# A hybrid decoder trunk on one core: the mLSTM matmuls of the sample tokens widened from 64 or 32 rows to 128

## The chip, the cores and the metric

The kernel runs on one core of one Trainium2 chip. The metric is the device time of one execution in microseconds (us). The core has five engines with instruction queues of their own: TensorE (PE in the profile; its weight loads are listed as PEld), VectorE (DVE), ScalarE (ACT), GpSimd (POOL) and SyncE (SP), which issues all the DMAs here.

## The reference

One decoder layer is computed for two groups of tokens with shared weights: a prompt of 256 tokens, and 8 samples with 8 new tokens each. So there are 320 tokens, of model width 2048, all in fp32.

```python
x1 = layer_norm(ALPHA * x + 0.5 * swiglu_ffn(x, ffn1_w1, ffn1_w3, ffn1_w2), ln1_g, ln1_b)
q, k, v, o, ig, fg, glu_a, glu_b, gate_a, gate_b = jnp.split(x1 @ w_in, SPLIT_IDX, axis=-1)
h_a, (C_new, n_new, m_new) = mlstm_branch(q, k, v, o, ig, fg, b_igate, b_fgate, mh_norm_g, C0, n0, m0, chunk)
h_b, conv_new = conv_branch(glu_a, glu_b, conv_buf, conv_w, conv_b, conv_ln_g, conv_ln_b)
mix = (sigmoid(gate_a) * h_a + sigmoid(gate_b) * h_b) @ w_out
x2 = layer_norm(ALPHA * x1 + mix, ln2_g, ln2_b)
y = layer_norm(ALPHA * x2 + 0.5 * swiglu_ffn(x2, ffn2_w1, ffn2_w3, ffn2_w2), ln3_g, ln3_b)
```

The part that the change touches is the mLSTM branch. For each of 4 heads (keys of 256, values of 512) and each chunk of tokens:

```python
s = einsum('bhtd,bhsd->bhts', q, k) * d            # d: masked decay, per sequence
num = einsum('bhts,bhsv->bhtv', s, v) + w_inter[..., None] * einsum('bhtd,bhdv->bhtv', q, C0)
qn = sum(s, axis=-1) + w_inter * einsum('bhtd,bhd->bht', q, n0)
h = num / maximum(abs(qn), exp(-m_t))[..., None]
C_new = w_c[..., None, None] * C0 + einsum('bhs,bhsd,bhsv->bhdv', w_k, k, v)
```

The prompt starts with an empty state. Each sample has a state `C0` of 256 x 512 numbers per head that is read, used, updated and written: 8 samples x 4 heads = 32 states of 512 KB in and 32 out.

## The kernel before

**Layout.** Activations are held transposed, 128 features x 320 tokens per tile. The weights stream from HBM in chunks of 8 blocks of 128 x 128 (`Stream`, lines 114 to 166; 512 KB each). Each chunk is split on the chip into a high part (`whi`, ACT, line 146) and a remainder (`wlo`, DVE, line 147), both of the type fp32r. A product of one weight block is three matmuls (`mm3`, lines 211 to 213): high x high, high x low, low x high. These three lines, called the weight matmuls below, write PSUM tiles `acc` of 128 x 320.

**Order.** `ffn`, `mixer`, `out_proj`, `ffn` follow each other. Inside `mixer` the weight matmuls of `w_in` run, and after each 4 blocks (12 matmuls) `tick` (line 188) takes one step of each of four lanes: lane 0 holds `gates` and then the four `head`s, lane 1 the norms, lanes 2 and 3 the convolutions of even and odd feature tiles, which run on DVE (line 611, one tap per step). A step ends at a `yield`. Where a later group needs a result, `drain` steps the lanes until it is there; the output gates `o` of a head wait so for that head (line 934). On top of this written order a scheduler of the framework rearranges instructions within each engine when the program is built. Its result is fixed: each engine runs its instructions in that order.

**One head** (`head`, line 647). `rb` holds four rows of factors broadcast over partitions. `sp` (line 677) are the products of keys and queries: two blocks of 128 prompt keys, and one block for the 64 sample tokens; `dt` is the masked decay, `pt` their product, and `ph`, `pl` its two parts. `tv` (line 712) are the transposed values, split into `vt`. `qn` (lines 731 to 749) is the normaliser. `cp` (line 762) makes the prompt's new state. `vst` and `kst` (lines 778 and 787) are values and weighted keys of the samples, each sample's 8 tokens and their remainder parts in a group of 32 partitions: 4 samples per `vst` tile, two tiles. Then for each of the 8 samples: `ip` (line 810, 4 matmuls) is the query times the old state, whose split parts are `chi` (ACT) and `clo` (DVE); `cps` (line 815, 2 matmuls) is the update of the state; DVE adds it to the old state (line 816); SP writes the state (line 820) and loads the one after next (line 657). State tiles `c0` come from a pool tag with three buffers, which the input tiles `xraw` (line 333) and some others also use. Last, `num` (line 833 through `mm3`, and line 836) adds the two parts of the numerator, for 4 blocks of 128 value columns.

The sample tokens have 64 rows where they are the contracted axis of a matmul (`num`, `qn`, and the last of the cumulative sums `bp`), and `cps` has 32:

```python
mm(cp, kst[r, g, j * P:(j + 1) * P], vst[g][r, :], start=True, stop=True, tile_position=(32 * i, 0))
```

The profile writes such a shape as rows*columns of the stationary operand: `32*128` here, `64*128` for `num` and `qn` of the samples, `128*32` for `ip`, `128*128` for the weight matmuls.

Of the kernel before, what the change touches and what calls it, by code (L numbers as in the profile page):

```python
# [35 lines left out]
SEGW = HIST + NS  # L36

# [131 lines left out]
class Kernel:  # L169
# [181 lines left out]
    def consts(self, cp):  # L351
        nc, a = self.nc, self.a
        cst = cp.tile([P, C_N], F32, name="cst")
        nc.sync.dma_start(out=cst, in_=a["cst"])
        self.ident = cst[:, C_ID:C_ID + P]
        self.tri = cst[:, C_TRI:C_TRI + P]
        self.btri = cst[:TS, C_BTRI:C_BTRI + TS]
# [48 lines left out]
        nc.vector.tensor_copy(self.sel, cst[:ROWS, C_SEL:C_SEL + H * P])  # L406
# [95 lines left out]
    def gates(self, g8):  # L502
# [144 lines left out]
    def head(self, h, q, k, v):  # L647
# [61 lines left out]
        for i, n in enumerate((P, P, TS)):  # L709
# [4 lines left out]
            nc.scalar.activation(x[0][:n], tv[:n], AF.Copy)  # L714
# [18 lines left out]
        for x in (ph, pl):  # L733
            mm(qn[:, SEQ:], one[:TS, :], x[:TS, 384:], start=x is ph, stop=False)
# [433 lines left out]
```

## Time and profile before

| | |
|---|---|
| times shown | 2999.9, 3186.01 and 2992.91 us, median 2999.9 us |
| profiled execution | 2996.54 us, its span 2994.8 us |
| mean granted TensorE clock | 0.988 |
| PE busy | 2940.2 us, 98% of the span, 19580 matmuls |
| DVE busy | 1893.9 us, 63% |
| ACT busy | 1340.8 us, 45% |
| DMA | 460.32 MB, mean 154 GB/s |

A row of a timeline gives the start from the beginning of the span and the duration, both in us. Matmuls overlap: the end of one lies behind the start of the next, and its end is modelled. What a matmul costs the stream is therefore the distance from its start to the start of the next. Rows of a table of stretches give, for each engine, the busy time in the stretch and the instructions that started or ran in it; `PEclk` is the granted clock of TensorE, 1.00 at full speed. Groups of instructions are `line engine operation out<-in, shape, xcount | busy us, mean ns of one | idle before`.

### The profile page before, as it was taken

What the parts mean: (1) busy time and instruction counts of PE and PEld (TensorE: products, weight loads), DVE (VectorE), ACT (ScalarE), POOL (GpSimd) and SP (SyncE); (2) the same over time, 40 slices, a digit from 0 to 9 for tenths busy, and PEclk for the clock granted to TensorE, in tenths of its full rate; (3) what the DMA queues carried; (4) which work ended last, traced back from release to release, by engine and by line L of the source; (5) the groups of instructions that cost most, each with busy time, mean ns of one, the idle gap of its engine ahead of it and who ended that gap; (6) DMA issues with size and microseconds to landing.
All of it is one profiled execution on the core that took longest, in us unless ns stands there. A gap on an engine that the chain in (4) does not pass through costs nothing.

```text
span 2994.8 us, 50339 instructions
## 1 busy us (share of the span) xinstructions
PE 2940.2 (98%) x19580; PEld 2883.3 (96%) x19580; DVE 1893.9 (63%) x3498; ACT 1340.8 (45%) x2392; POOL 70.7 (2%) x76
## 2 busy tenths in 40 slices
PE   9999999999999999999999989999999999999997
PEld 9999999999998998989999889999999999999997
DVE  5544444444459999979989876578544444444447
ACT  5434433433445545545544545445433433433444
POOL 0100000000000000000000000200100000000001
PEclk9999999999999999999999989999999999999999
DMA  6444444444444456464555634444444444444443
GB/s 220 152 150 148 150 153 148 149 150 152 148 149 140 127 162 211 151 201 124 175 184 154 210 109 141 148 148 134 151 152 148 148 152 151 148 150 152 149 148 106
DMA packets 163136, 460.32 MB, mean 154 GB/s; under 512 B 50128, under 2 KB 52944, under 8 KB 162896
## 3 DMA queue, kind: packets, MB, share of 16 engines
q1 hardware_dynamic: 162896, 457.10, 47.2%
q8 instruction: 153, 2.51, 0.4%
q14 instruction: 87, 0.71, 0.1%
HBM read 433.29 MB, written 23.74 MB: 153 GB/s over the span
## 4 chain that ended last, share of the span: by engine, by line
PE 96%; DVE 2%; DMA 1%; ACT 1%; issue 0%; DVEq 0%; SPq 0%; ACTq 0%
PE acc L211 31%; PE acc L212 31%; PE acc L213 31%; PE ip L810 1%; PE cps L815 1%; DMA out_C_s<-c 0%; PE num L836 0%; PE num L211 0%; DVE wlo L147 0%; DMA c<-in_C 0%; PE num L213 0%; PE num L212 0%; DVE z L1083 0%; DVE z L473 0%; DVE xl L488 0%; ACT th L246 0%
## 5 line engine op out<-in xcount | busy, mean ns | idle before, releaser
L147 DVE TENSOR_TENSOR wlo<-wraw,whi 128x512 fp32r<-128x512 f32 x1568 | 1080.9, 691 | 924.4 <-ACT whi L146 918.8
L146 ACT ACTIVATE whi<-wraw 128x512 fp32r<-128x512 f32 x1568 | 987.7, 631 | 1453.4 <-PE acc L212 1342.8
L211 PE MATMUL acc<-xh,whi 128*128 128x320 f32 x4480 | 1392.7, 311 | 20.5 <-ACT th L246 9.6
L212 PE MATMUL acc<-xl,whi 128*128 128x320 f32 x4480 | 1390.7, 311 | 6.6 <-DVE xl L488 6.6
L213 PE MATMUL acc<-xh,wlo 128*128 128x320 f32 x4480 | 1387.6, 311 | 1.8 <-DVE wlo L147 1.8
L211 PEld LDWEIGHTS acc<-xh,whi 128*128 128x128 f32 x4480 | 847.4, 189 | 30.0 <-ACT th L246 10.5
L212 PEld LDWEIGHTS acc<-xl,whi 128*128 128x128 f32 x4480 | 847.2, 189 | 15.4 <-DVE xl L488 7.9
L213 PEld LDWEIGHTS acc<-xh,wlo 128*128 128x128 f32 x4480 | 844.8, 189 | 10.4 <-issue 3.9
L211 PE MATMUL acc<-hh,whi 128*128 128x320 f32 x1408 | 433.9, 309 | 0.3 <-ACT whi L146 0.3
L212 PE MATMUL acc<-hl,whi 128*128 128x320 f32 x1408 | 433.7, 309 | 0.0
L213 PE MATMUL acc<-hh,wlo 128*128 128x320 f32 x1408 | 432.5, 309 | 0.0
L211 PEld LDWEIGHTS acc<-hh,whi 128*128 128x128 f32 x1408 | 264.4, 188 | 0.6 <-ACT whi L146 0.6
L212 PEld LDWEIGHTS acc<-hl,whi 128*128 128x128 f32 x1408 | 264.2, 188 | 0.0
L213 PEld LDWEIGHTS acc<-hh,wlo 128*128 128x128 f32 x1408 | 263.9, 188 | 0.0
L611 DVE SCALAR_TENSOR_TENSOR cy<-pu,cw,cy 128x256 f32<-128x256 f32 x480 | 221.2, 476 | 1.0
L435 DVE SCALAR_TENSOR_TENSOR z<-acc,z 128x320 f32<-128x320 f32 x128 | 62.5, 488 | 54.5 <-PE acc L213 52.8
L211 PE MATMUL acc<-mh,whi 128*128 128x320 f32 x256 | 79.1, 309 | 0.0
L212 PE MATMUL acc<-ml,whi 128*128 128x320 f32 x256 | 79.0, 309 | 0.0
L213 PE MATMUL acc<-mh,wlo 128*128 128x320 f32 x256 | 78.7, 309 | 0.0
L313 POOL TENSOR_TENSOR z<-xh,xl 128x320 f32<-128x320 f32 x48 | 60.7, 1272 | 632.3 <-DVE h L425 351.7
L425 DVE TENSOR_TENSOR h<-s,acc 128x320 f32<-128x320 f32 x86 | 42.0, 488 | 52.2 <-ACT s L423 52.2
L423 ACT ACTIVATE s<-acc 128x320 f32<-128x320 f32 x86 | 37.7, 438 | 69.2 <-PE acc L213 69.2
(285 smaller groups left out, 1673.6 us busy)
## 6 DMA issues: line engine op xcount, KB each, us to landing
wraw<-in_wst SPq DMA_DIRECT2D x783, 512.0 KB, 3.3
c<-in_C SPq DMA_DIRECT2D x32, 512.0 KB, 4.1
out_C_s<-c SPq DMA_DIRECT2D x32, 512.0 KB, 4.8
out_yT<-z SPq DMA_DIRECT2D x16, 160.0 KB, 1.8
out_C_p<-cn SPq DMA_DIRECT2D x4, 512.0 KB, 2.9
us<-in_cache SPq DMA_DIRECT2D x16, 120.0 KB, 3.7
out_conv_s<-us SPq DMA_DIRECT2D x16, 120.0 KB, 6.0
xraw<-in_xT SPq DMA_DIRECT2D x3, 480.0 KB, 5.3
```

The source lines that it names most:

```text
L146: nc.scalar.activation(hi, raw, AF.Copy)
L147: nc.vector.tensor_tensor(out=lo, in0=raw, in1=hi.bitcast(F32), op=ALU.subtract)
L211: mm(ps, hi, xh, start=first, stop=False)
L212: mm(ps, hi, xl, start=False, stop=False)
L213: mm(ps, lo, xh, start=False, stop=last)
L313: self.nc.gpsimd.tensor_tensor(out=t, in0=hi.bitcast(F32), in1=lo.bitcast(F32), op=ALU.add)
L423: nc.scalar.activation(s, accs[2 * j], AF.Silu)
L425: nc.vector.tensor_tensor(out=hh, in0=s, in1=accs[2 * j + 1], op=ALU.mult)
L435: nc.vector.scalar_tensor_tensor(out=z[m], in0=ps, scalar=0.5 / ALPHA, in1=z[m], op0=ALU.mult, op1=ALU.add)
L611: nc.vector.scalar_tensor_tensor(out=yp, in0=pu[:, w:w + SEQ], scalar=self.cw[:, i, w:w + 1], in1=yp, op0=ALU.mult, op1=ALU.add)
L810: mm(ip[:32, :], qc[j][:, bs], x, start=j == 0 and n == 0, stop=j == 1 and n == 1)
L815: mm(cp, kst[r, g, j * P:(j + 1) * P], vst[g][r, :], start=True, stop=True, tile_position=(32 * i, 0))
```

## The change

The 64 sample tokens are no longer a third tile of 64 rows. The third tile is now the last 128 of the 320 tokens (`TILES = (0, P, T - P)`): 64 prompt tokens that also stand in the second tile, and the 64 sample tokens. The mask `btri` becomes a 128 x 128 tile that is zero outside the samples' corner, so that the prompt's rows in the third tile count for nothing. So `sp`, `dt`, `pt`, `ph`, `pl`, `tv`, `vt`, the samples' part of `qn` and `num`, and the gates' small products work on 128 partitions; several pairs of instructions (384 columns on 128 partitions, 64 columns on 64) become one of 448 columns. For `cps`, four constant tiles `kst` of 128 x 512 are zeroed once in `consts`; each head's `ks` is copied by four ACT instructions of 32 partitions into the band of the tile that belongs to the sample, and the matmul takes all 128 rows of that tile and of `vst`. The columns of all matmuls and the count of `cps`, `qn` and `num` matmuls stay. `ip` (128 rows, 32 columns) and `pb` (36 rows, line 663) are unchanged. To make room in SBUF, the constant `sel` is loaded through a tile `selraw` of the tag `c0` rather than as part of `cst`; `btri` has a DMA of its own.

```diff
+TILES = (0, P, T - P)
...
     def consts(self, cp):
-        cst = cp.tile([P, C_N], F32, name="cst")
-        nc.sync.dma_start(out=cst, in_=a["cst"])
+        cst = cp.tile([P, C_SEL], F32, name="cst")
+        nc.sync.dma_start(out=cst, in_=a["cst"][:, :C_SEL])
+        sel = self.mp.tile([ROWS, H * P], F32, tag="c0", name="selraw", bufs=3)
+        nc.sync.dma_start(out=sel, in_=a["cst"][:ROWS, C_SEL:])
...
-        self.btri = cst[:TS, C_BTRI:C_BTRI + TS]
+        self.btri = cp.tile([P, P], F32, name="btri")
+        nc.vector.memset(self.btri, 0.0)
+        nc.sync.dma_start(out=self.btri[P - TS:, P - TS:], in_=a["cst"][:TS, C_BTRI:C_BTRI + TS])
...
-        nc.vector.tensor_copy(self.sel, cst[:ROWS, C_SEL:C_SEL + H * P])
+        nc.vector.tensor_copy(self.sel, sel)
+
+        self.kst = []
+        for i in range(NB // 2):
+            t = cp.tile([P, 2 * DQK], F32R, name=f"kst{i}")
+            nc.vector.memset(t.bitcast(F32), 0.0)
+            self.kst.append(t)
...
     def head(self, h, q, k, v):
-            nc.vector.tensor_scalar(dt[:n, c0_:c1], mb[:n, t0:t0 + c1 - c0_], self.acol[:n, i, h:h + 1], 0.0, op0=ALU.subtract, op1=ALU.max)
+        blocks = ((0, 256, 0, 0), (256, 384, P, 1), (384, 448, SEQ, 2))
+        for c0_, c1, t0, i in blocks:
+            nc.vector.tensor_scalar(dt[:, c0_:c1], mb[:, t0:t0 + c1 - c0_], self.acol[:, i, h:h + 1], 0.0, op0=ALU.subtract, op1=ALU.max)
...
-                mm(sp[:n, c0_:c1], k[j][:, s0:s0 + n], q[j][:, t0:t0 + c1 - c0_], start=j == 0, stop=j == 1)
-        nc.scalar.activation(dt[:, :384], dt[:, :384], AF.Exp, scale=-1.0)
-        nc.scalar.activation(dt[:TS, 384:], dt[:TS, 384:], AF.Exp, scale=-1.0)
+                mm(sp[:, c0_:c1], k[j][:, TILES[i]:TILES[i] + P], q[j][:, t0:t0 + c1 - c0_], start=j == 0, stop=j == 1)
+        nc.scalar.activation(dt, dt, AF.Exp, scale=-1.0)
...
-        for i, n in enumerate((P, P, TS)):
+        for i, o in enumerate(TILES):
             tv = self.sm([P, DV], "tv")
             for j in range(4):
-                nc.tensor.transpose(tv[:n, j * P:(j + 1) * P], v[j][:, i * P:i * P + n], self.ident)
+                nc.tensor.transpose(tv[:, j * P:(j + 1) * P], v[j][:, o:o + P], self.ident)
...
-            mm(qn[:, SEQ:], one[:TS, :], x[:TS, 384:], start=x is ph, stop=False)
+            mm(qn[:, SEQ:], one, x[:, 384:], start=x is ph, stop=False)
...
-        kst = mp.tile([P, 2, DQK], F32R, tag="kst", name="kst", bufs=1)
-        nc.scalar.activation(kst, ks, AF.Copy)
+        for i, x in enumerate(self.kst):
+            r = slice(32 * i, 32 * (i + 1))
+            nc.scalar.activation(x[r], ks[r].rearrange("p g d -> p (g d)"), AF.Copy)
...
-                mm(cp, kst[r, g, j * P:(j + 1) * P], vst[g][r, :], start=True, stop=True, tile_position=(32 * i, 0))
+                at = g * DQK + j * P
+                mm(cp, self.kst[i][:, at:at + P], vst[g], start=True, stop=True)
...
-                (2, TS, slice(SEQ, T), slice(384, 448), True, False),
+                (2, slice(SEQ, T), slice(384, 448), True, False),
             ):
-                self.mm3(num[:, t], [x[:n, f] for x in vt[c]], ph[:n, cs], pl[:n, cs], first, last)
+                self.mm3(num[:, t], [x[:, f] for x in vt[c]], ph[:, cs], pl[:, cs], first, last)
```

The scheduler gives each engine another order at many places. Two of them follow.

The DMA queue of SP at the start of the program. `xraw` are the inputs (320 columns for one feature tile, 640 for two, 960 for three), `wraw` the weight chunks, `us` the cached inputs of the convolution, the rest are constants. Before:

```order
6 L134 DMA wraw<-in_wst 128x1024
7 L334 DMA xraw<-in_xT 128x640
8 L134 DMA wraw<-in_wst 128x1024 x2
9 L334 DMA xraw<-in_xT 128x640
10 L354 DMA cst<-in_cst 128x872
11 L361 DMA par<-in_par 128x160
12 L334 DMA xraw<-in_xT 128x960
18 L334 DMA xraw<-in_xT 128x960
19 L134 DMA wraw<-in_wst 128x1024 x3
20 L599 DMA us<-in_cache 128x8x30 x2
21 L134 DMA wraw<-in_wst 128x1024
22 L334 DMA xraw<-in_xT 128x960
```

The same place of the same queue now:

```order
6 L136 DMA wraw<-in_wst 128x1024 x3
7 L356 DMA cst<-in_cst 128x360
8 L364 DMA btri<-in_cst 64x64
9 L336 DMA xraw<-in_xT 128x640
10 L368 DMA par<-in_par 128x160
12 L336 DMA xraw<-in_xT 128x640
14 L336 DMA xraw<-in_xT 128x960
18 L136 DMA wraw<-in_wst 128x1024 x3
19 L610 DMA us<-in_cache 128x8x30 x2
20 L136 DMA wraw<-in_wst 128x1024
21 L336 DMA xraw<-in_xT 128x960 x2
22 L358 DMA selraw<-in_cst 36x512
```

The fourth input transfer (feature tiles 3 and 4) now stands behind two more weight chunks, `cst` and `btri`; the one of tiles 10 to 12 now stands behind four weight chunks and both `us`, beside the last one.

PE at the end of the samples' loop of the second head (head 1), where the program drains that head for its output gates. Before, samples 6 and 7 and the first `num`:

```order
8674 L810 MATMUL ip<-chi,cat 32x512
8675 L212 MATMUL acc<-xl,whi 128x320
8676 L213 MATMUL acc<-xh,wlo 128x320
8677 L815 MATMUL cps<-vst_13685,kst 128x512
8678 L810 MATMUL ip<-clo,cat 32x512
8679 L810 MATMUL ip<-chi,cat 32x512
8680 L810 MATMUL ip<-clo,cat 32x512
8681 L815 MATMUL cps<-vst_13685,kst 128x512
8682 L810 MATMUL ip<-chi,cat 32x512
8683 L815 MATMUL cps<-vst_13685,kst 128x512 x2
8684 L810 MATMUL ip<-clo,cat 32x512
8687 L211 MATMUL num<-ph,vt 128x256
```

The same end of the loop now, from the last `cps` of sample 6 on:

```order
8643 L826 MATMUL cps<-vst_13688,kst_221 128x512
8644 L215 MATMUL acc<-xh,wlo 128x320
8645 L213 MATMUL acc<-xh,whi 128x320
8655 L214 MATMUL acc<-xl,whi 128x320
8656 L215 MATMUL acc<-xh,wlo 128x320
8657 L820 MATMUL ip<-chi,cat 32x512
8658 L826 MATMUL cps<-vst_13688,kst_223 128x512
8659 L820 MATMUL ip<-clo,cat 32x512
8660 L820 MATMUL ip<-chi,cat 32x512
8661 L820 MATMUL ip<-clo,cat 32x512
8662 L826 MATMUL cps<-vst_13688,kst_223 128x512
8663 L213 MATMUL num<-ph,vt 128x256
```

Before, `ip` and `cps` of samples 6 and 7 follow each other with no weight matmul between the last `ip` of sample 6 (8680) and the first of sample 7 (8682). Now the last `ip` of sample 6 is instruction 8624, and 30 weight matmuls stand between it and the first `ip` of sample 7 (8657); counted in weight matmuls, the `ip` of samples 0 to 6 of this head moved forward by 28 to 38 of them. In the other three heads `ip` and `cps` moved by at most 25 weight matmuls either way.

More of the change, by code (lines that the diff above doesn't have):

```diff
@@ L511, in gates @@
         tp = self.sm([P, 3, 2 * H], "gt")
-        for i, n in enumerate((P, P, TS)):
-            mm(tp[:n, i, :], grow[:, i * P:i * P + n], self.pick_g, start=True, stop=True)
+        for i, o in enumerate(TILES):
+            mm(tp[:, i, :], grow[:, o:o + P], self.pick_g, start=True, stop=True)
         gt = mp.tile([P, 3, 2 * H], F32, tag="gt", name="gt", bufs=1)
-        nc.vector.memset(gt, 0.0)
         gb = self.gbias.unsqueeze(1).to_broadcast([P, 3, 2 * H])
-        for sl in (np.s_[:, 0:2, :], np.s_[:TS, 2:3, :]):
-            nc.vector.tensor_tensor(out=gt[sl], in0=tp[sl], in1=gb[sl], op=ALU.add)
+        nc.vector.tensor_tensor(out=gt, in0=tp, in1=gb, op=ALU.add)
         ig, fg = gt[:, :, 0:H], gt[:, :, H:2 * H]
@@ L532, in gates @@
         mm(bp[:, 1, :], self.tri, lf[:, 1, :], start=False, stop=True)
-        mm(bp[:TS, 2, :], self.btri, lf[:TS, 2, :], start=True, stop=True)
+        mm(bp[:, 2, :], self.btri, lf[:, 2, :], start=True, stop=True)
         b = mp.tile([P, 3, H], F32, tag="b", name="b", bufs=1)
         acol = mp.tile([P, 3, H], F32, tag="acol", name="acol", bufs=1)
-        for sl in (np.s_[:, 0:2, :], np.s_[:TS, 2, :]):
-            nc.vector.tensor_copy(b[sl], bp[sl])
-            nc.vector.tensor_tensor(out=acol[sl], in0=ig[sl], in1=b[sl], op=ALU.subtract)
+        nc.vector.tensor_copy(b, bp)
+        nc.vector.tensor_tensor(out=acol, in0=ig, in1=b, op=ALU.subtract)
         yield
@@ L541, in gates @@
         ap_, bp_ = self.sm([H, T], "arow"), self.sm([H, T], "brow")
-        for i, n in enumerate((P, P, TS)):
-            nc.tensor.transpose(ap_[:, i * P:i * P + n], acol[:n, i, :], self.ident[:n, :n])
-            nc.tensor.transpose(bp_[:, i * P:i * P + n], b[:n, i, :], self.ident[:n, :n])
+        for x, src in (ap_, acol), (bp_, b):
+            for i in range(2):
+                nc.tensor.transpose(x[:, i * P:(i + 1) * P], src[:, i, :], self.ident)
+            mm(x[:, SEQ:], src[:, 2, :], self.ident[:, P - TS:], start=True, stop=True)
         arow, brow = row("arow"), row("brow")
@@ L680, in head @@
+        nc.scalar.activation(dt, dt, AF.Exp, scale=-1.0)
         yield
-        for c0_, n, msk in ((0, P, self.tri), (256, P, self.tri), (384, TS, self.btri)):
+        for c0_, msk in ((0, self.tri), (256, self.tri), (384, self.btri[:, P - TS:])):
             w = msk.shape[1]
-            nc.vector.tensor_tensor(out=dt[:n, c0_:c0_ + w], in0=dt[:n, c0_:c0_ + w], in1=msk, op=ALU.mult)
+            nc.vector.tensor_tensor(out=dt[:, c0_:c0_ + w], in0=dt[:, c0_:c0_ + w], in1=msk, op=ALU.mult)
         yield
@@ L694, in head @@
+        nc.vector.tensor_tensor(out=pl, in0=pt, in1=ph.bitcast(F32), op=ALU.subtract)
         kw = [self.t("kw") for _ in range(2)]
@@ L827, in head @@
             num = self.sm([P, T], "num")
-            for c, n, t, cs, first, last in (
-                (0, P, slice(0, SEQ), slice(0, SEQ), True, False),
-                (1, P, slice(P, SEQ), slice(256, 384), False, True),
-                (2, TS, slice(SEQ, T), slice(384, 448), True, False),
+            for c, t, cs, first, last in (
+                (0, slice(0, SEQ), slice(0, SEQ), True, False),
+                (1, slice(P, SEQ), slice(256, 384), False, True),
+                (2, slice(SEQ, T), slice(384, 448), True, False),
             ):
-                self.mm3(num[:, t], [x[:n, f] for x in vt[c]], ph[:n, cs], pl[:n, cs], first, last)
+                self.mm3(num[:, t], [x[:, f] for x in vt[c]], ph[:, cs], pl[:, cs], first, last)
             for g in range(2):
```

16 lines of the change are left out of this document (6 added, 10 removed).

## The prediction

> **What bounds the kernel now.** I read the page first: its engines and the chain that ended last.
>
> ```profile
> span 2994.8 us, 50339 instructions
> PE 2940.2 (98%) x19580; PEld 2883.3 (96%) x19580; DVE 1893.9 (63%) x3498; ACT 1340.8 (45%) x2392; POOL 70.7 (2%) x76
> PE 96%; DVE 2%; DMA 1%; ACT 1%; issue 0%; DVEq 0%; SPq 0%; ACTq 0%
> ```
>
> PE is the end of everything: 96% of the chain. Next, a table of stretches: the rows that begin at 1143, 1296, 1476 and 1680 are the samples' loops of heads 0 to 3, those at 1335, 1531 and 1732 the ends of heads 1 to 3, and 1356 lies between two loops.
>
> ```profile
> core 0: us, PE busy (x) PEld busy (x) DVE busy (x) ACT busy (x) POOL busy (x), PEclk, DMA share, GB/s
> 1143.00:1198.00 55.00, 55.00 (x313) 45.88 (x312) 48.83 (x85) 27.34 (x48) 0.00 (x0) 1.00 0.76 234
> 1296.00:1335.00 39.00, 39.00 (x215) 31.35 (x215) 32.74 (x61) 17.62 (x31) 0.12 (x1) 1.00 0.68 215
> 1335.00:1358.00 23.00, 18.66 (x71) 15.87 (x71) 16.60 (x30) 5.65 (x12) 0.12 (x1) 0.55 0.52 151
> 1356.00:1476.00 120.00, 120.00 (x808) 117.81 (x807) 111.85 (x242) 65.86 (x132) 0.25 (x2) 0.99 0.50 150
> 1476.00:1531.00 55.00, 55.00 (x316) 46.20 (x316) 48.26 (x83) 27.97 (x50) 0.12 (x1) 1.00 0.74 234
> 1531.00:1553.00 22.00, 22.00 (x134) 21.23 (x134) 15.94 (x34) 4.97 (x9) 0.12 (x1) 0.84 0.30 97
> 1680.00:1732.00 52.00, 52.00 (x292) 42.70 (x291) 44.27 (x75) 26.31 (x48) 0.00 (x0) 1.00 0.71 235
> 1732.00:1754.00 22.00, 22.00 (x126) 21.41 (x125) 14.96 (x32) 5.31 (x11) 0.00 (x0) 0.77 0.22 76
> ```
>
> In the four loops PE is never idle, but it gets through few instructions: 313 in 55 us, against 808 in the 120 us between loops, 5.7 per us against 6.7. DVE stands close behind PE everywhere. At 1335 PE idles for 4.3 us, and the granted clock falls; it falls after 1531 and 1732 too, with PE busy.
>
> **What a narrow matmul costs.** PE's timeline in a loop, one `cps` among weight matmuls:
>
> ```profile
> 1165.37 0.31 PE L212 MATMUL acc<-xl,whi 128*128 128x320 f32 x1
> 1165.61 0.49 PE L815 MATMUL cps<-vst,kst 32*128 32x512 f32 x1
> 1166.03 0.42 PE L213 MATMUL acc<-xh,wlo 128*128 128x320 f32 x1
> 1166.28 0.31 PE L211 MATMUL acc<-xh,whi 128*128 128x320 f32 x1
> 1166.43 0.31 PE L212 MATMUL acc<-xl,whi 128*128 128x320 f32 x1
> ```
>
> A weight matmul follows the one before it after 0.15 us (1166.28 to 1166.43). Around `cps` the distances are 0.24, 0.42 and 0.25: from 1165.37 to 1166.43 pass 1.06 us, of which three weight matmuls would take 0.44. One `cps` costs 0.62 us. A 512-column matmul with all 128 rows stands elsewhere, six in a row:
>
> ```profile
> 1103.17 0.31 PE L213 MATMUL acc<-xh,wlo 128*128 128x320 f32 x1
> 1103.32 0.39 PE L211 MATMUL cp<-vt,kt 128*128 128x512 f32 x1
> ...
> 1104.47 0.39 PE L213 MATMUL cp<-vt,kt 128*128 128x512 f32 x1
> 1104.70 0.31 PE L211 MATMUL acc<-xh,whi 128*128 128x320 f32 x1
> ```
>
> 1.53 us less one weight matmul (0.15), divided by 6, is 0.23 us each. So a padded `cps` should save 0.39 us.
>
> ```profile
> L815 PE MATMUL cps<-vst,kst 32*128 32x512 f32 x64 | 30.9, 495 | 0.0
> ```
>
> There are 64. The order puts 54 of them alone; ten stand in five pairs, whose cost of entering and leaving is paid once, so I count a pair as one: 59 x 0.39 = 23.0 us. As bounds I take 59 x 0.28 = 16.5 (the third distance, 0.25, stays as it is) and 64 x 0.39 = 25.
>
> **The smaller matmuls.** `num` of the samples, and the samples' part of `qn`, have 64 rows:
>
> ```profile
> 1533.93 0.27 PE L212 MATMUL num<-pl,vt 128*128 128x128 f32 x1
> 1534.04 0.28 PE L213 MATMUL num<-ph,vt 128*128 128x128 f32 x1
> 1534.25 0.29 PE L211 MATMUL num<-ph,vt 64*128 64x64 f32 x1
> 1534.38 0.27 PE L212 MATMUL num<-pl,vt 64*128 64x64 f32 x1
> 1534.49 0.27 PE L213 MATMUL num<-ph,vt 64*128 64x64 f32 x1
> 1534.70 0.63 PE L836 MATMUL num<-cst,st 128*128 128x32 f32 x4
> ...
> 1097.13 0.29 PE L734 MATMUL qn<-ph,one 64*128 64x64 f32 x1
> 1097.27 0.27 PE L734 MATMUL qn<-pl,one 64*128 64x64 f32 x1
> 1097.47 0.42 PE L211 MATMUL acc<-xh,whi 128*128 128x320 f32 x1
> ```
>
> From 1534.04 to 1534.70 are four distances of 0.21, 0.13, 0.11 and 0.21, where full rows go at 0.11 (1533.93 to 1534.04): 0.66 - 0.44 = 0.22 us, for 16 blocks (4 heads x 4) 3.5 us. `qn`'s distances are 0.14 and 0.20; at 0.11 that is 0.12 less, with as much again for entering and for the matmul behind, as at `cps`: 0.25 x 4 heads = 1.0 us. Together 4.5 (bounds 3 and 6). `sp` and `tv` had 128 rows already, with 64 columns; more columns may cost up to nothing or bring a little: 0.
>
> **ACT and DVE.** `kst` is four ACT copies instead of one, each at most as long as a copy of 512 columns (0.58 us, half of the 1.15 for two `chi` below): 3 x 0.58 x 4 heads = 7 us more ACT, in a loop where ACT works 27 of 55 us, and the first `cps` needs only the first copy. Were that cover gone, the weight halves behind it on ACT would be 1.7 us late per head. On DVE the merged instructions save a few short ones; the four zeroings of 128 x 512 at the start have no row, and at that copy's 0.58 us would be 2.3 us among the first splits, which PE's new order there bridges by taking four high parts before the first low part. I take 0 for both, and put 1 us into the start's upper bound.
>
> **Head 1's wait** rests on the moved order:
>
> ```profile
> 1162.76 1.15 ACT L796 ACTIVATE chi<-c 128x512 fp32r<-128x512 f32 x2 [0.86 <-DMA c<-in_C]
> 1168.96 0.39 PE L810 MATMUL ip<-chi,cat 128*32 128x512 f32 x1
> ...
> 1335.06 0.50 PE L815 MATMUL cps<-vst,kst 32*128 32x512 f32 x1
> 1339.21 1.15 ACT L796 ACTIVATE chi<-c 128x512 fp32r<-128x512 f32 x2 [3.46 <-DMA c<-in_C]
> 1339.89 0.63 PE L810 MATMUL ip<-chi,cat 128*32 128x512 f32 x1 [4.33 <-ACT chi L796]
> ```
>
> PE had nothing left but `ip` of sample 7, and its state landed late. Now 30 weight matmuls, 30 x 0.15 = 4.4 us, stand in that gap, and the earlier samples, whose writes release the load, moved forward as well. But `cps` is shorter, so PE arrives earlier. I take 3.6 us off and leave 0.7; bounds 0 and 4.3.
>
> **The start.** Two input transfers moved behind weight chunks on SP:
>
> ```profile
> 9.74 0.82 ACT L261 ACTIVATE xh<-xraw 128x320 fp32r<-128x320 f32 x2
> 10.88 1.15 ACT L146 ACTIVATE whi<-wraw 128x512 fp32r<-128x512 f32 x2 [0.32 <-DMA wraw<-in_wst]
> 12.32 0.61 PE L211 MATMUL acc<-xh,whi 128*128 128x320 f32 x3
> 28.86 1.19 ACT L261 ACTIVATE xh<-xraw 128x320 fp32r<-128x320 f32 x3 [1.74 <-DMA xraw<-in_xT]
> ```
>
> Feature tiles 3 and 4 were split at 9.74 and first used at 12.32. One chunk of 512 KB came 1.14 us behind them, so two chunks and 200 KB of constants make them 2.7 us later: 12.4, and with the split (0.41 each part) 13.3, a stall of 1 us. Each feature tile then takes 12 matmuls, 1.76 us, so tile 10 is due at 12.3 + 7 x 1.76 + 1 = 25.7. It now has the place of the transfer that was ready at 28.86; that would be a stall of 3.6 with its split. As 480 KB less stand ahead of it (1.1 us), and SP reaches it sooner, I take 1.5. Behind it on SP wait the last inputs, `selraw` (which needs a `c0` buffer that is free by then) and the weight chunks, which run two to three chunks ahead. Sum +2.5, bounds 0.5 and 5.6 (1 + 3.6 + 1).
>
> **The sum.** The profiled execution took 2996.5 us (span 2994.8), beside a median of 2999.9 and a lowest of 2992.9 of the times shown. 2996.5 - 23.0 - 4.5 - 3.6 + 2.5 = 2967.9, predicted 2968. With the bounds of the terms alone: 2996.5 - 16.5 - 3 - 0 + 5.6 = 2983, and 2996.5 - 25 - 6 - 4.3 + 0.5 = 2962.
>
> **Rivals.**
>
> *DVE becomes the bound of the loops.* Sixteen `cps` save 6.2 us in a loop where DVE idles 6.2 (55 - 48.83), 6.3, 6.7 and 7.7 us. The highest share it holds beside a full PE over a long stretch is 111.85 / 120 = 93.2%. If it can't pass that, the four loops, 201 us with 174.1 of DVE, shrink to 186.8: 14.2 gained instead of 23. Time 2977. Against it: weight halves are made ahead, and DVE can catch up between loops. 21%.
>
> *The clock stays up.* With 0.84 over 22 us and 0.77 over 22 us, TensorE ran at half clock for 7 and 10 us (2 x 0.16 and 2 x 0.23 of 22) behind the loops of heads 2 and 3, among `num`s. At most half of that, 8.5 us, is lost; I take 7. At head 1, 0.55 over 23 us is 20.7 us at half clock, 16 beside the wait: at most 8, I take 6. If tighter `num`s and the shorter wait keep the clock: 2968 - 13 = 2955. The Trainium skill ("TensorE: Matmul & The Clock Gate", Part 1) has a gate that goes between half and full by the activity in windows of about 3.4 us; the trace agrees in kind, and by it this case is the likelier the more a `num` block is compressed. Against it: a block of `num` loses only 0.22 us. 12%.
>
> *The states come too late in every head (slower).* In head 0 a `chi` pair was done at 1163.91 and used at 1168.96, 5.05 us later; a loop gets 6.2 us shorter, and loads wait for writes on SP. If PE runs into the load at the end of heads 0, 2 and 3 as it did in head 1, each pays that head's price, 4.3 of waiting and 6 of half clock: 2996.5 - 27.5 + 2.5 + 3 x 10.3 = 3002. It decides where slack shrinks by all of 5 us; against it, writes and loads follow `cps` and move forward with it. 6%.
>
> *Width is not what costs.* `cps` may be dear for what stands around it, a switch of operands, and stay so with full rows; then 23 goes: 2991. The six `cp` in a row don't show a lone one. The trace's 0.62 against 0.23 speaks against it. 7%. The Trainium skill (same page, "Why this matters for your kernels") says that a lone 32-row matmul takes as long as a 128-row one and gains only by running beside others on other rows; by that rule padding gains nothing and gives up the overlap inside the pairs.
>
> **Chances.** My forecast 54%, with 2962 to 2983; then 21, 12, 6 and 7%. The first three, 87%, lie between 2955 and 2983; 2992.9 and 2999.9 lie 3.5 us to either side of the profiled time, so the range is 2952 to 2986. 2% of 2996.5 is 60 us, about what a measurement here can tell from no change; no case reaches 2937 or 3056: 0.98 for the middle, 0.01 on each side.
>
> **What would show it.** PE's timeline: 0.15 into and 0.23 out of each `cps`, no 0.25 behind it; `num` at 0.11 throughout; loops about 6 us shorter with PE busy and DVE at 97% or more; no PE wait over 1 us before the `ip` of head 1's last sample; a stall of 1 us near 12 and 1.5 near 26. I am wrong if `cps` keeps a distance of 0.4, if PE idles in the loops, or if waits of several us arise before `ip` in other heads.

## The result and the profile after

The changed kernel took 2962.7 us (median of four runs, 2961.7 to 2973.7), the kernel before 2998.2 beside it (median of four). The ratio of the fast runs alone, without the one of 3186.01 us of before, is 0.9897, 95% interval 0.9880 to 0.9914. The time lies in the range, 5 us under the 2968.0 predicted, and under the 2% that counts as a change. The profiled execution took 2962.41 us (span 2960.6), 34.1 less than that of before.

The page of the changed kernel, engines and chain:

```profile
span 2960.6 us, 50364 instructions
PE 2900.5 (98%) x19582; PEld 2867.5 (97%) x19582; DVE 1892.2 (64%) x3491; ACT 1346.7 (45%) x2396; POOL 70.6 (2%) x76
PE 93%; DMA 2%; DVE 2%; ACT 1%; issue 0%; DVEq 0%; SPq 0%; ACTq 0%
```

PE is still the end of everything, with two matmuls more than before; DVE and ACT do as much as they did. DMA's share of the chain went from 1% to 2%, 1% for loads of states and 1% for their stores.

PE's timeline of the changed kernel in head 0's loop, a `cps` alone among weight matmuls and one with an `ip` behind it:

```profile
1174.61 0.31 PE L213 MATMUL acc<-xh,whi 128*128 128x320 f32 x1
1174.76 0.40 PE L826 MATMUL cps<-vst,kst 128*128 128x512 f32 x1
1174.99 0.30 PE L214 MATMUL acc<-xl,whi 128*128 128x320 f32 x1
1175.14 0.31 PE L215 MATMUL acc<-xh,wlo 128*128 128x320 f32 x1
...
1168.02 0.39 PE L826 MATMUL cps<-vst,kst 128*128 128x512 f32 x1
1168.25 0.39 PE L820 MATMUL ip<-chi,cat 128*32 128x512 f32 x1
1168.48 0.31 PE L213 MATMUL acc<-xh,whi 128*128 128x320 f32 x1
```

Around the lone one the distances are 0.15, 0.23 and 0.15: `cps` adds 0.23 us, where it added 0.62. `num` of head 2, PE's timeline:

```profile
1515.93 0.28 PE L215 MATMUL num<-ph,vt 128*128 128x128 f32 x1
1516.05 0.24 PE L213 MATMUL num<-ph,vt 128*128 128x64 f32 x1
1516.13 0.28 PE L214 MATMUL num<-pl,vt 128*128 128x64 f32 x1
1516.24 0.28 PE L215 MATMUL num<-ph,vt 128*128 128x64 f32 x1
1516.35 0.61 PE L847 MATMUL num<-cst,st 128*128 128x32 f32 x4
```

Four distances make 0.42, before 0.66: 0.24 saved a block, 0.22 predicted.

The loops of the four heads whole, from the first `ip` to the first `num`; the table of stretches, columns as in the prediction, of before and then of the changed kernel:

```profile
1133.40:1199.50 66.10, 66.10 (x386) 56.38 (x385) 58.49 (x104) 34.54 (x62) 0.00 (x0) 1.00 0.73 223
1286.80:1342.90 56.10, 51.77 (x285) 41.46 (x285) 46.13 (x87) 24.53 (x43) 0.25 (x2) 0.95 0.66 209
1466.70:1533.50 66.80, 66.80 (x392) 57.16 (x392) 58.73 (x105) 34.66 (x62) 0.12 (x1) 1.00 0.71 224
1672.20:1733.00 60.80, 60.80 (x352) 51.09 (x351) 51.55 (x89) 31.30 (x57) 0.00 (x0) 1.00 0.65 218
```

```profile
1136.70:1198.80 62.10, 59.91 (x382) 55.63 (x381) 54.40 (x98) 34.55 (x63) 0.00 (x0) 1.00 0.72 228
1279.40:1332.70 53.30, 51.57 (x322) 46.47 (x320) 46.34 (x89) 28.80 (x51) 0.12 (x1) 1.00 0.65 221
1452.90:1515.40 62.50, 62.50 (x401) 58.66 (x400) 57.81 (x106) 37.67 (x70) 0.25 (x2) 1.00 0.72 232
1647.30:1704.50 57.20, 56.02 (x355) 51.66 (x355) 51.11 (x91) 33.12 (x62) 0.00 (x0) 1.00 0.72 229
```

They are 4.0, 2.8, 4.3 and 3.6 us shorter. PE, busy all through three of them before, now idles 2.2, 1.7 and 1.2 us in heads 0, 1 and 3. DVE's share is 87 to 92%. The idle time, PE's timeline of the changed kernel, with what it waited for in brackets:

```profile
13.68 0.85 PE L213 MATMUL acc<-xh,whi 128*128 128x320 f32 x4 [1.12 <-ACT xh L263]
1160.10 0.41 PE L820 MATMUL ip<-chi,cat 128*32 128x512 f32 x1 [1.35 <-ACT st L821]
1330.24 0.42 PE L820 MATMUL ip<-chi,cat 128*32 128x512 f32 x1 [1.42 <-ACT chi L806]
1368.35 0.41 PE L213 MATMUL acc<-xh,whi 128*128 128x320 f32 x1 [0.84 <-ACT k L927]
1692.70 0.42 PE L820 MATMUL ip<-chi,cat 128*32 128x512 f32 x1 [0.53 <-ACT chi L806]
```

The wait of 4.33 us in head 1 became 1.42, and shorter ones came up in heads 0 and 3.

**One sum for all kernels.** To set the kernels of this study against each other I split PE's time, from the first matmul's start to the last one's, in each profiled execution. Each distance from a matmul to the next is set against the median distance of the same two shapes at full clock over all fourteen traces. What fits is *matmul work* (the three distances behind a matmul of fewer rows count as they are, so the price of a change of rows is in it); what goes beyond is the *rest*, PE idle or at half clock. The rest of the loops, of `num` together with all that lies between the loops, and of the drain behind head 3 (to 1830 us) stand apart; the other parts of the rest (the start, the stretch ahead of head 0, the last layer) are in its total only.

| profiled execution | total | matmul work | rest | loops | num and between | drain |
|---|---|---|---|---|---|---|
| before | 2974.4 | 2911.5 | 62.9 | 5.7 | 14.8 | 18.9 |
| changed | 2940.3 | 2884.8 | 55.5 | 6.7 | 5.1 | 18.1 |
| cps alone | 2960.9 | 2889.5 | 71.4 | 11.9 | 14.1 | 18.1 |
| all but cps | 2962.4 | 2906.7 | 55.6 | 2.2 | 9.2 | 18.5 |
| cps on 32 rows | 2960.0 | 2907.9 | 52.0 | -0.2 | 6.5 | 18.0 |
| cps on 64 rows | 2958.4 | 2908.2 | 50.3 | -0.1 | 6.4 | 17.9 |
| before, cps twice | 2976.9 | 2926.6 | 50.3 | -0.2 | 13.3 | 12.4 |
| num on 64 rows | 2956.8 | 2888.4 | 68.4 | 5.3 | 14.0 | 23.7 |
| four buffers | 2957.9 | 2884.7 | 73.1 | 6.9 | 13.3 | 21.6 |
| cps alone, four buffers | 2957.2 | 2889.7 | 67.5 | 4.0 | 9.8 | 22.6 |
| keys zeroed on GpSimd | 2940.3 | 2884.6 | 55.6 | 8.2 | 8.6 | 15.6 |
| and pb on 128 rows | 2941.0 | 2883.1 | 57.9 | 6.2 | 8.2 | 18.5 |
| and four buffers | 2940.7 | 2883.2 | 57.5 | 4.8 | 10.3 | 17.7 |
| and st on DVE | 2942.3 | 2883.2 | 59.0 | 6.7 | 9.0 | 17.9 |

The change took 26.7 us of matmul work and 7.4 of the rest. Each row is one execution, and executions of one kernel lay up to 12 us apart (the changed kernel 2961.7 to 2973.7, with granted clocks of 0.993 to 0.990), so a few us in a column of the rest need not come from the kernel.

### The profile page after: what moved, and what is told of

The parts are those of the page before. It is cut to its first block, busy times and chain, and to the rows that moved or that the text cites. A ratio compares the mean times of both kernels' runs of the same rounds, so it can differ in the third digit from the quotient of the medians.

```text
span 2960.6 us, 50364 instructions
## 1 busy us (share of the span) xinstructions
PE 2900.5 (98%) x19582; PEld 2867.5 (97%) x19582; DVE 1892.2 (64%) x3491; ACT 1346.7 (45%) x2396; POOL 70.6 (2%) x76
## 4 chain that ended last, share of the span: by engine, by line
PE 93%; DMA 2%; DVE 2%; ACT 1%; issue 0%; DVEq 0%; SPq 0%; ACTq 0%
PE acc L213 30%; PE acc L214 30%; PE acc L215 30%; DMA c<-in_C 1%; DMA out_C_s<-c 1%; PE ip L820 1%; DVE wlo L149 0%; PE cps L826 0%; PE sp L689 0%; ACT whi L148 0%; PE num L847 0%; DMA xraw<-in_xT 0%; DVE z L1094 0%; DVE z L486 0%; DVE c L827 0%
```

## The experiments

My theory after the result: the price lies in each change of row count on PE, and what the change gained beyond the count (some 6 us) is half-clock time that the short `num` had brought, less what late states gave back. Rivals: the new order or the constant key tiles carry the gain; a matmul of few rows is itself slow; and, for the part beyond the count, chance of the order.

**One part each.** `cps` alone on 128 rows, put into the kernel before, with the four zeroed tiles and the split constants that it needs (not printed here):

```diff
-        kst = mp.tile([P, 2, DQK], F32R, tag="kst", name="kst", bufs=1)
-        nc.scalar.activation(kst, ks, AF.Copy)
+        for i, x in enumerate(self.kst):
+            r = slice(32 * i, 32 * (i + 1))
+            nc.scalar.activation(x[r], ks[r].rearrange("p g d -> p (g d)"), AF.Copy)
...
-                mm(cp, kst[r, g, j * P:(j + 1) * P], vst[g][r, :], start=True, stop=True, tile_position=(32 * i, 0))
+                at = g * DQK + j * P
+                mm(cp, self.kst[i][:, at:at + P], vst[g], start=True, stop=True)
```

> Before, with the cps matmuls alone on 128 rows (constant zero-padded keys, the split of the constants that makes room for them); gates, logits, ph/pl, values and num keep their 64 and 32 rows. Theory (it is the rows of cps): 64 cps at 0.23 us in place of 0.62 are 64 x 0.39 = 25 us less, the start keeps about 1.7 us more, so about 2973 us against 2996.5. For the half-speed stretches of the granted clock at the ends of heads 1, 2 and 3, which are gone or moved in the changed kernel, there are two readings: if the short-row num matmuls bring them, they stay here and it is 2973 to 2976; if the stream with fewer changes of width before them takes them away, they go here too and it is 2965 to 2968. Rival (the other edits, or the order that they give, carry the gain): within 8 us of before.

Measured: 2985.7 us, ratio 0.9972 (0.9959 to 0.9984). Neither theory's number. The count itself holds, the matmul work fell by 22.0 us; but the rest rose by 8.5. PE's timeline of this kernel at the end of head 1:

```profile
1330.97 0.42 PE L819 MATMUL ip<-chi,cat 128*32 128x512 f32 x1 [2.32 <-ACT chi L805]
1333.60 0.80 PE L825 MATMUL cps<-vst,kst 128*128 128x512 f32 x1 [0.67 <-ACT st L820]
1338.23 0.64 PE L819 MATMUL ip<-chi,cat 128*32 128x512 f32 x1 [3.83 <-ACT chi L805]
```

PE came to samples 6 and 7 ahead of their states (ACT's `chi` waited for their loads), and the granted clock is at half from 1332.2 to 1342.4 and from 1345.8 to 1356.1. The start is worse by 4.0 us.

The complement is the changed kernel with the two edits above taken back and without the four zeroed tiles:

> The changed kernel with cps and its keys as before (32 rows), all else changed: gates, logits, ph/pl, values, num and qn on 128 rows, constants split. Theory: 16 num x 0.22 and 1.0 for qn are 4.5 us less, 0.9 of it at least; about 1 to 1.7 us more at the start: 2993 us, or 2986 if the num matmuls' rows are what brings the half-speed stretches at the ends of heads 1 to 3. Rival (the order and the other edits carry the gain): 2963 to 2972.

Measured: 2982.3 us, 0.9957 (0.9942 to 0.9971). Matmul work 4.8 us less than before (4.5 counted; 0.4 of it is one more pair of `cps`, 58 changes for 59), the rest 7.3 less. The half-clock stretches at the ends of heads 2 and 3 are gone here and stand in the other kernel (1530.2 to 1537.0 and 1724.7 to 1735.0). The two parts save 22.0 and 4.8 us of matmul work, the whole 26.7: that adds up. The rests, +8.5 and -7.3, don't add up to the whole's -7.4.

**Width alone.** Same tiles, copies and order of code as in the changed kernel; each `cps` reads 32 rows of the padded keys, or 64:

```diff
-                mm(cp, self.kst[i][:, at:at + P], vst[g], start=True, stop=True)
+                mm(cp, self.kst[i][r, at:at + P], vst[g][r, :], start=True, stop=True, tile_position=(32 * i, 0))
```

> The changed kernel with one edit: each cps reads only the 32 rows of the padded keys that are not zero, and the same 32 rows of the values. Same tiles, same copies, same memory, same order. Theory (rows of the matmul): 64 x 0.39 = 25 us more than the changed kernel, 2987 us, a cps again 0.62 us with what stands behind it. Rival (the constant key tiles, their copies or the order are what helps): 2963 us. In between if a part of the 25 us was given back to waits in the changed kernel: the waits of 1.1 to 1.7 us before ip would be gone here, and it is 2982.

```diff
-                mm(cp, self.kst[i][:, at:at + P], vst[g], start=True, stop=True)
+                r = slice(64 * (i // 2), 64 * (i // 2 + 1))
+                mm(cp, self.kst[i][r, at:at + P], vst[g][r, :], start=True, stop=True, tile_position=(r.start, 0))
```

> The changed kernel with cps on the 64 rows that hold its 32 (zeros in the other 32). If the price is paid for each change of row count, whatever it is: about 0.62 us a cps as with 32 rows, 60 x 0.39 = 23 us of TensorE work, and 2981 us as the narrow variant measured. If it falls with the rows left out: about 0.4 us, 2972 us. If 64 rows cost nothing: 2963 us.

Measured: 2981.6 us with 32 rows, 0.9954 (0.9939 to 0.9969), and 2980.8 with 64, 0.9952 (0.9938 to 0.9967). The matmul work rose by 23.1 and 23.4 us, for 60 changes (56 alone, four pairs) 0.39 each. PE's matmuls stand in the changed kernel's order in both, so neither the order nor the constant tiles bring that part of the gain. PE's timeline with 64 rows:

```profile
1174.98 0.30 PE L213 MATMUL acc<-xh,whi 128*128 128x320 f32 x1
1175.22 0.49 PE L827 MATMUL cps<-vst,kst 64*128 64x512 f32 x1
1175.64 0.41 PE L214 MATMUL acc<-xl,whi 128*128 128x320 f32 x1
1175.89 0.31 PE L215 MATMUL acc<-xh,wlo 128*128 128x320 f32 x1
```

0.24, 0.42, 0.25, to the hundredth those of 32 rows: the price doesn't go by the rows left out. In both kernels the waits of the loops are gone, as the slower loop gives the states time; so of 60 x 0.39 = 23.4 us, 5 came back (18.9 and 18.1 measured between the medians).

**Change or slowness.** Before, with each `cps` issued twice in a row; the product is computed twice, with the same result:

```diff
-                mm(cp, kst[r, g, j * P:(j + 1) * P], vst[g][r, :], start=True, stop=True, tile_position=(32 * i, 0))
+                for _ in range(2):
+                    mm(cp, kst[r, g, j * P:(j + 1) * P], vst[g][r, :], start=True, stop=True, tile_position=(32 * i, 0))
```

> Before, with each cps matmul issued twice in a row (same operands, same result). Theory (the cost is the change of width into and out of a 32-row matmul): the second one of a pair costs a plain 0.23 us, so 64 x 0.23 = 15 us more, 3011 us. Rival (a 32-row matmul is itself slow): the second costs 0.62 us as well, 64 x 0.62 = 40 us more, 3036 us. If TensorE has idle time in the loops that hides it, less than 10 us more.

Measured: 2999.5 us, 1.0016 (1.0006 to 1.0025): 5 us, not 15. The trace shows why the total misleads:

```profile
1166.14 0.31 PE L212 MATMUL acc<-xl,whi 128*128 128x320 f32 x1
1166.37 0.73 PE L816 MATMUL cps<-vst,kst 32*128 32x512 f32 x2
1167.03 0.42 PE L213 MATMUL acc<-xh,wlo 128*128 128x320 f32 x1
1167.29 0.31 PE L211 MATMUL acc<-xh,whi 128*128 128x320 f32 x1
```

Into the pair 0.23, out of it 0.66, where one `cps` took 0.42: the second costs 0.24, what a full-row matmul of that size costs. So a 32-row matmul among its like isn't slow; the change is. The matmul work rose by 15.1 us (14.7 expected); the rest fell by 12.6, as the 4.33 us wait of head 1 is gone and the drain is 6.5 us shorter. The Trainium skill ("TensorEngine Tiling (Array Packing)", Key Properties) says that a change of tiling mode drains the array. The traces agree for a change of rows: 0.39 us for a change and back among full-row matmuls. The Trainium skill ("TensorE: Matmul & The Clock Gate", "Why this matters for your kernels") takes a lone 32-row matmul for as long as a 128-row one; here that holds inside a pair, not for a lone one.

**The clock.** The changed kernel with only `num`'s three matmuls over a sample's own sources on 64 rows:

```diff
+                if c < 2:
                     self.mm3(num[:, t], [x[:, f] for x in vt[c]], ph[:, cs], pl[:, cs], first, last)
+                else:
+                    lo = slice(P - TS, P)
+                    for n, (x, y) in enumerate(((0, ph), (0, pl), (1, ph))):
+                        mm(num[:, t], vt[c][x][lo, f], y[lo, cs], start=n == 0, stop=False, tile_position=(P - TS, 0))
```

> The changed kernel with only num's three matmuls over a sample's own sources back on 64 rows (cps, qn, logits and the rest stay on 128). The row changes alone: 16 x 0.22 = 3.5 us more, 2966 us. Reading A of the clock (short-row matmuls among the num bring the half-speed stretches that stand at the end of heads 2 and 3 in every kernel with 64-row num and in none without): the stretches come back there, about 2 us more each, 2970 us. Reading B (they come from something else that the change moved): none there, 2966 us.

Measured: 2974.9 us, 0.9930 (0.9913 to 0.9946), 12 us over the changed kernel, beyond both readings. PE's matmuls stand in the same order as there. Matmul work +3.6 as counted; rest +12.9 in the profiled execution, which at 2978.9 us was the longest of four; for the shortest, 2971.6, the same sum leaves 5.6. The stretches of heads 2 and 3 around `num`, first the changed kernel, then this one (the column before the last two is the granted clock):

```profile
1515.00:1521.00 6.00, 6.00 (x54) 6.00 (x53) 5.96 (x15) 0.83 (x2) 0.00 (x0) 1.00 0.50 178
1704.00:1726.00 22.00, 22.00 (x164) 22.00 (x163) 19.00 (x42) 7.79 (x17) 0.00 (x0) 1.00 0.39 133
```

```profile
1520.00:1525.40 5.40, 5.40 (x43) 5.06 (x42) 4.65 (x11) 0.18 (x1) 0.00 (x0) 1.00 0.55 196
1525.40:1532.20 6.80, 6.80 (x28) 6.62 (x28) 4.81 (x11) 0.63 (x1) 0.00 (x0) 0.50 0.01 4
1712.00:1716.50 4.50, 4.50 (x36) 4.20 (x35) 4.20 (x10) 0.49 (x2) 0.00 (x0) 1.00 0.76 269
1716.50:1726.80 10.30, 10.30 (x42) 10.05 (x43) 6.35 (x15) 1.26 (x2) 0.00 (x0) 0.50 0.00 2
```

PE is busy throughout, and yet, with `num` on short rows, it drops to half clock 4 to 6 us after the first of them, in heads 1 to 3; with full rows in none. The same division runs through all fourteen kernels at heads 2 and 3: all five with 64-row `num` have a stretch that begins 5 to 8 us after the first `num` of head 2, and four of them one at head 3 (not `cps` alone with four buffers); of the nine with full rows none has either. Reading A stands, undersized: with 1 to 2 us at each `num`, as much behind each, and 5.6 in the drain, which begins at half clock, it comes to 13 instead of 4 in this execution.

What the busy time doesn't show, a count of columns does. From 30 to 2900 us all changes of the clock in a trace lie on a grid of 3.413 us (to 0.002). In one cell of that grid the stream of weight matmuls passes some 7400 columns (320 in each 0.147 us). Of the 11575 cells at full clock in the fourteen traces, 84 are followed by half clock. I counted the columns of the matmuls that start in each: the 84 lie below 3100 and the other cells above it, with 13 exceptions in all. Among the cells that overlap a `num`, on 64 rows or on 128, there is none: all with at most 3072 columns are followed by half clock, and none with 3200 or more is. At heads 2 and 3 the emptiest cells over `num` hold 3072 and 2944 columns here and 3904 and 3840 in the changed kernel, with the same matmuls in the same order. At head 0 here the emptiest holds 3776, and the clock stays up. That thin cells are the cause is argued from this sorting; a count of columns weighted by rows has 10 exceptions, so whether rows count too stays open.

**Late states.** A state's buffer is loaded again only after its store. Three buffers made that a chain; so the changed kernel with four:

```diff
-                c0[b] = mp.tile([P, 2, DV], F32, tag="c0", name="c0", bufs=3)
+                c0[b] = mp.tile([P, 2, DV], F32, tag="c0", name="c0", bufs=4)
...
-        pt = mp.tile([P, 448], F32, tag="pt", name="pt", bufs=1)
+        pt = dt
...
-            tc.tile_pool(name="t", bufs=72) as tp,
+            tc.tile_pool(name="t", bufs=71) as tp,
```

> The changed kernel with four buffers for the states in place of three (room made by multiplying logits and scores in place and by one row tile less). A state's buffer is loaded again only after the state that used it was stored: in the changed kernel sample 2 of head 1 was stored at 1304.7, sample 5 loaded at 1309.1 and stored at 1325.4, so 6.9 us a sample, and TensorE's loops there have 2.5, 2.3 and 1.5 us of waits before ip and cps in heads 0, 1 and 3. Theory (late states hold the loops back once cps is cheap): the 6.3 us go, 2956 us. Rival (the copies that ACT queues, or DVE, hold the loops back): 2962 us, waits before ip as before.

Measured: 2975.1 us, 0.9938 (0.9923 to 0.9953): slower than the changed kernel. The waits before `ip` did go, in all heads. In their place stands one wait before the very last `cps` of head 1, PE's row, and ACT's two rows that hold it:

```profile
1337.97 0.80 PE L826 MATMUL cps<-vst,kst 128*128 128x512 f32 x1 [6.49 <-ACT st L821]
```

```profile
1336.16 1.15 ACT L806 ACTIVATE chi<-c 128x512 fp32r<-128x512 f32 x2 [5.78 <-DMA c<-in_C]
1337.33 0.58 ACT L821 ACTIVATE st<-ip 32x512 f32<-32x512 f32 x1
```

ACT takes `chi` of head 2's first state ahead of the copy of head 1's last `ip`, and that state was loaded only at 1331.4. Half clock follows (1334.2 to 1344.4). The stretch from 60 to 955 us lost 4.2 us too; it lost nothing where four buffers go with all 72 row tiles (below). Both theories are half right: the buffers removed the waits that they should, and ACT's order took the place. The same four buffers for `cps` alone:

> Before with cps alone on 128 rows and four state buffers. With three buffers this edit gained 9 us where the count of 59 row changes at 0.39 gives 23; its trace has 11.3 us of waits in the loops of heads 0 and 1 (before: 5.6), 4 us more at the start. Theory (the gain was given back to late states): the 11 us go, 2974 us. Rival (it was given back to DVE or ACT, or cps saves less than counted): 2983 to 2986 us.

Measured: 2980.8 us, 0.9956 (0.9941 to 0.9971), in between. The rest of its loops fell from 11.9 to 4.0, so late states had taken some 8 us of that gain; 4.2 were lost again in the first layer and 4.5 in the drain.

**Looking for a better version.** First the start: the four padded key tiles zeroed on GpSimd.

```diff
-            nc.vector.memset(t.bitcast(F32), 0.0)
+            nc.gpsimd.memset(t.bitcast(F32), 0.0)
```

> The changed kernel with the four padded key tiles zeroed on GpSimd in place of DVE. In the changed kernel their four memsets stand at the head of DVE (1.47 to 4.05 us) and the first xl follows at 5.05 us, at 3.56 in the variant without those tiles. Theory (DVE's head sets the start): the stall of 1.43 us at 12.2 us goes, 1.5 to 2 us less, 2961 us, if the order behind it stays. Rival (the split constants set the start): 2963 us, stall as before. All kernels so far differ by up to 20 us in TensorE's idle and half-speed time with the same matmuls, so either reading is judged by the start's rows, not by the total.

DVE's timeline at the start, of the changed kernel and then of this one:

```profile
1.47 1.56 DVE L418 MEMSET kst<- 128x512 f32 x3
2.96 0.56 DVE L390 TENSOR_SCALAR one<-ones 128x128 fp32r<-128x128 f32 x4
3.57 0.48 DVE L418 MEMSET kst<- 128x512 f32 x1
4.21 0.91 DVE L597 MEMSET parts<- 36x1024 f32 x1 [0.15 <-DMA wraw<-in_wst]
5.05 0.42 DVE L264 TENSOR_TENSOR xl<-xraw,xh 128x320 fp32r<-128x320 f32 x1
```

```profile
2.41 0.86 DVE L390 TENSOR_SCALAR one<-ones 128x128 fp32r<-128x128 f32 x4
3.80 0.49 DVE L264 TENSOR_TENSOR xl<-xraw,xh 128x320 fp32r<-128x320 f32 x1 [0.53 <-ACT xh L263]
```

The first split comes 1.25 us earlier. SP's queue moved with it; the fourth input transfer in the changed kernel, and in this one:

```profile
6.15 0.53 SPq L336 DMA_DIRECT2D xraw<-in_xT  x1
```

```profile
4.32 0.33 SPq L336 DMA_DIRECT2D xraw<-in_xT  x1
```

The rest of the start fell from 3.8 to 2.2 us, with no stall at 12: the theory's part. The time was 2968.1 us, 0.9907 (0.9892 to 0.9922), not told apart from the changed kernel, since the order behind moved as well: head 1 now waits up to 1.86 us before `ip` and is at half clock from 1327.2 to 1347.7. On top of it, `pb` on 128 rows:

```diff
-        self.sel = cp.tile([ROWS, H * P], F32R, name="sel")
+        self.sel = cp.tile([P, H * P], F32R, name="sel")
+        nc.gpsimd.memset(self.sel.bitcast(F32), 0.0)
...
-        parts = mp.tile([ROWS, R_N], F32R, tag="parts", name="parts", bufs=1)
-        nc.vector.memset(parts.bitcast(F32), 0.0)
+        parts = mp.tile([P, R_N], F32R, tag="parts", name="parts", bufs=1)
+        nc.gpsimd.memset(parts.bitcast(F32), 0.0)
```

> As that one, and the four pairs of pb matmuls on 128 rows in place of 36 (the gate rows and the selector padded with zeros, zeroed on GpSimd). If each change of row count costs what it costs around cps: 4 x 0.39 = 1.6 us less TensorE work, 2959.5 us in all. Rival: the pair already hides in its wait for the rows (1.75 us in head 0), nothing gained there, 2961 us.

2964.5 us, 0.9901 (0.9884 to 0.9917). Matmul work 1.5 us less (1.6 expected); the rest is 2.3 us more. Then four buffers again, all 72 row tiles kept, and last the copy of the last `ip` on DVE:

```diff
-        w = mp.tile([P, KD, 2, 2 * H], F32R, tag="wgp", name="wgp", bufs=1)
+        w = mp.tile([P, KD, 2, 2 * H], F32R, tag="c0", name="wgp", bufs=4)
...
-            x = mp.tile([P, TS], F32, tag="qs", name="qs", bufs=2)
+            x = mp.tile([P, TS], F32, tag="qs", name="qs", bufs=1)
```

> The variant with keys zeroed on GpSimd and pb on 128 rows, and four state buffers, the row tiles kept at 72 this time (room from the logits multiplied in place, the gate weights in a state buffer and one qs in place of two). The waits before ip and cps in head 1 (1.1, 0.4 and 1.4 us) and the half-speed stretch at 1328 to 1345 us that begins 3 us after them are worth 11.2 us there, 2.4 in the changed kernel. Theory (late states bring both): 9 to 11 us less, 2954 us. Rival (with four buffers the last cps of head 1 waits for ACT, which holds on the next head's first state, as in the other variant with four buffers, 6.5 us): 2960 to 2966 us.

```diff
-            nc.scalar.activation(st[r, g, :], ip[:32, :], AF.Copy)
+            if b + 1 < NB:
+                nc.scalar.activation(st[r, g, :], ip[:32, :], AF.Copy)
+            else:
+                nc.vector.tensor_copy(st[r, g, :], ip[:32, :])
```

> As that one, and the copy of the last sample's ip from PSUM goes to DVE, so that it can't stand on ACT behind the next head's chi. If that wait (6.5 us before the last cps of head 1 in the first variant with four buffers) is what four buffers cost: no wait over 1 us at the end of head 1, no half-speed stretch there, 2953 us. Rival (another operation takes its place): 2960 us or more.

2963.2 us, 0.9899 (0.9884 to 0.9914), and 2964.1 us, 0.9901 (0.9884 to 0.9917): the rivals' numbers. At the end of head 1 PE still waits, up to 2.8 us for ACT's copies of `ip`, and half clock still follows (1328.7 to 1339.0, and 1326.9 to 1347.4). None of these is faster than the changed kernel.

## Why the prediction was right, point by point

- **`cps`**, 59 changes at 0.39, -23.0: right. Alone it took 22.0 us of matmul work; with 32 or 64 rows put back it gave 23.1 and 23.4. The rival that width isn't the cost is refuted by those two kernels, which change nothing else.
- **`num` and `qn`**, -4.5: right, 4.8 measured in the kernel without the `cps` part (0.4 of it from `cps`), 3.6 for `num` alone.
- **ACT and DVE at 0**: right as totals (DVE 1893.9 to 1892.2 us, ACT 1340.8 to 1346.7). The DVE zeroings, for which I kept 1 us in a bound, were 1.6 us of the start.
- **The start**, +2.5 from stalls of 1 us near 12 and 1.5 near 26: 1.7 measured, 1.4 of it PE's stall before 13.68 and only 0.3 near 26. The cause that I gave, input transfers behind weight chunks, fits, but what put them there were the zeroings on DVE: with those on GpSimd the transfer is issued at 4.32, not 6.15, and the stall goes.
- **Head 1's wait**, -3.6: its direction was right, with 1.4 us left, not 0.7. But PE's idle time in heads 0 and 3, 2.2 and 1.2 us, was in no term. It is the slower rival in small: slack there shrank until PE met the state in places, without the half clock that I priced in, and the loops' rest came out 1.0 us higher, where I had 3.6 lower.
- **DVE as the bound**: didn't happen, since the loops were 2.8 to 4.3 us shorter, not 6, with DVE at 87 to 92%, not 97%. I had held the loops' contents fixed; but the order put 43 more weight matmuls into the four loops (1247 for 1204), 6.3 us that left other places.
- **The clock**: this is the step that failed. I left it out of the sum and gave it 12% as a rival. The rest of `num` and what lies between fell from 14.8 to 5.1 us, 9.7 where the sum had nothing and the rival 13. Some 6 of it stood at heads 2 and 3 (7 in the rival), where the rows of `num` bring half clock; some 4 at head 1 (6 in the rival), where half clock had begun at 1337.4, in PE's wait and ahead of the first `num` (1342.89), so that part goes with the shorter wait, as far as one trace shows. My argument against it, that a block loses only 0.22 us, is what failed: with 0.24 us less a block the emptiest cells over `num` at heads 2 and 3 went from 3008 and 2944 columns to 3904 and 3840, across the mark.

The sum was 28.6 us less; 34.1 came. Of the 5.5 between them, the terms of matmul work gave 0.8 less than counted, the start 0.8 more, the loops 4.6 less; the clock (with the waits that lie between loops) gave 9.7 more, and the other stretches 0.4 (-0.8 in the drain, -0.7 in the last layer, +1.1 ahead of head 0).

How far the rest can be foretold stays open. Over kernels with nearly the same matmuls it lies between 50 and 73 us: what a wait at the end of head 1 costs depends on whether half clock follows. The table of stretches around that wait, of the changed kernel, where none follows, and of the one with keys zeroed on GpSimd, where half clock begins at 1327.2:

```profile
1327.20:1330.60 3.40, 1.98 (x13) 1.57 (x12) 2.15 (x5) 1.05 (x2) 0.00 (x0) 1.00 0.85 343
```

```profile
1322.00:1327.20 5.20, 3.03 (x15) 1.70 (x13) 3.59 (x7) 3.99 (x7) 0.00 (x0) 1.00 0.85 314
```

PE is busy 58% of either, over unequal lengths. By columns they part: the cell of the grid ahead of 1327.2 has 2560, below the mark, and the changed kernel's cells from 1327.2 to 1337.4 have 3904, 3488 and 3616. How the grid lies against the program differs from trace to trace, so a wait of the same length can fall into one cell or two.

## What to carry to other kernels

A 512-column matmul of fewer rows standing alone in a stream of full ones paid 0.39 us here for the change, whether it had 32 or 64 rows (three 64-column ones in a row, in `num`, paid 0.24 together): pad it with zeros, or put the narrow ones next to each other, and count changes rather than matmuls. Judge such an edit by PE's matmul work in the trace: the saving was there to within a few tenths in every kernel, while waits and the clock took back 8.5 of 22.0 us in one profiled execution and added 7.4 to 26.7 in another. When a loop on PE gets shorter, look for the chain that is next, here the three buffers that are stored and loaded in turn, before the saving is booked.

## What was not expected of the hardware

- **Half clock without idle PE.** A few short-row matmuls among full ones were enough, with PE busy in every row (4.50 of 4.50 us, then clock 0.50 for 10.3). The stretches were 3.41, 6.83, 10.24, 13.65, 17.07 and 20.48 us long, multiples of 3.41. The Trainium skill ("TensorE: Matmul & The Clock Gate", Part 1) gives that window, 3413 ns, and an idle one as the cause of the drop; the length agrees, but the windows here were not idle by PE's busy time. By the count above they were thin: at most 3072 columns, some 40% of what weight matmuls pass.
- **Columns are free of it.** `ip`, with 128 rows and 32 columns, goes in and out at 0.23 us (1168.02 to 1168.25 and 1168.25 to 1168.48), like any full matmul of 512 columns, and the distance behind is 0.14 (to 1168.62): no price for fewer columns shows.
